# An encoder trunk's token mixer: conv output product as three one-pass products, attention block 1's last steps at fixed places, the LayerNorm's transposes in one row

## The chip, the cores and the metric

The kernel runs on one NeuronCore of a Trainium2 chip. The core has a matrix engine (TensorE, PE, with its weight loads PEld), a vector engine (VectorE, DVE), a scalar engine (ScalarE, ACT), a third elementwise engine (GpSimd, POOL), a queue for data movement (SyncE, SP), and DMA engines that bring data from memory (HBM). The engines run side by side, each works through its own list of instructions in order, and they wait for each other by semaphores. The metric is the device time of one launch in microseconds (us); less is better.

## What is computed

Two encoder layers on 256 tokens of width 1024, all float32. Cut to what the change touches:

```python
h = x + 0.5 * swiglu(rms_norm(x, norm_ffn1), w_ffn1_in, w_ffn1_out)
u = rms_norm(h, norm_mix)
q, k, v, c, g = split(u @ w_in)             # 512, 128, 128, 1024, 2048 columns
y_attn = window_attention(q, k, v, sink, rel_bias) @ w_attn_out     # 512 -> 1024
c = c_val * sigmoid(c_gate)                 # 512 channels
c = depthwise_conv(c, conv_w) + conv_b      # 31 taps
c = silu(layer_norm(c, conv_ln_g, conv_ln_b))
y_conv = c @ w_conv_out                     # 512 -> 1024
h = h + (sigmoid(g_attn) * y_attn + sigmoid(g_conv) * y_conv) @ w_o
h = h + 0.5 * swiglu(rms_norm(h, norm_ffn2), w_ffn2_in, w_ffn2_out)
x = h + (p @ w_pe_proj) * sigmoid(rms_norm(h, norm_pe) @ w_pe_gate)
```

The hidden width of swiglu is 2816. Nearly all of the arithmetic is products of 256 tokens with large weights.

## The kernel before

**Products.** Activations lie with their channels on the 128 partitions and the 256 tokens along the free dimension. A float32 product is run in one of two ways. The usual one (`mm3`, L312) splits both operands into a high part, rounded to the one-pass type fp32r, and a low part, the rest; it adds three one-pass products for each tile of 128 input channels: high by high (L318), high weights by low activations (L319), low weights by high activations (L320). The other way (`products`, L859, its matmul on L863) multiplies the float32 operands as they are; it is used for the attention output (tiles `ps_ao`), whose activation `o` isn't split, and for the conv output (`ps_co`), whose activation `y` isn't split.

**Weights.** The class `Weights` streams them. A load of up to 1 MB goes through SP into one of four buffers (`raw`, RAW_BUFS). From it come pieces ("specs"): ACT casts the high part (`w_hi`, L103), DVE takes the difference (`w_lo`, L104), into one of seven pairs of buffers. `get()` hands the next piece to the product and prepares up to LOOK = 6 pieces ahead, less `rest`. A raw spec has no preparation: its product reads the raw buffer, which is held until then.

**Order.** Each instruction has a priority by its place in the program (and offsets: `ws.lag` puts the weights' preparation 100 places later, `background` the taps of the convolution 800); from these and the dependencies a scheduler makes a fixed list for each engine. `tc.keep_in_program_order` ties an instruction to the one written ahead of it on its engine. `ws.later(n, fn)` calls a step when the n-th next piece of weights is fetched.

**The mixer** (`mix`, twice in a run) projects u to the conv branch (two halves times a sigmoid, into `cpad`), keys, values and queries, then 16 gate tiles in 8 pairs (`ps_g`, evicted by DVE on L844). The 31 taps for each of four channel groups run on DVE (L614) between other work. Attention goes in two blocks of 128 queries: `scores` (products, then the softmax), `attend` for each of two heads' groups (8 transposes into `ps_pt` on L807, copied by ACT to `pTs` on L811) and `gather` (`ps_o` on L819, copied to `o` on L827). `ws.later` puts these steps between the gate tiles.

Then come four groups of the attention output `attn_out` (16 matmuls into `ps_ao`, evicted by DVE on L873); among them the LayerNorm of `y`: `ln_by_token` turns y to tokens on partitions (8 transposes, `ps_yt`, L885), takes the statistics (L887, L888, L891) and normalises (`yn`, L894); `ln_by_channel` turns back (`ps_yc`, L904), and ACT applies Silu into `y` (L908). Four groups of the conv output `conv_out` follow; each is multiplied by its gate (L935), added to the attention branch (L936), and split into `ym_h` (ACT, L453) and `ym_l` (DVE, L454). The product with w_o (`ps_wo`) ends in `x` (DVE, L954); from each of its 8 tiles ACT makes the square (L408, which POOL sums on L409) and `xf0h` (L441), and DVE `xf0l` (L442): the two parts of the next FFN's input, whose products are `ps_gu`. In layer 1 the names are `xf1h` and `xf1l`.

## Time and profile before

| | |
|---|---|
| median of three runs | 1104.88 us (1104.81 to 1105.29) |
| the profiled execution | 1104.41 us |
| its span on the core | 1102.6 us |
| PE busy | 1087.8 us (99%), 9082 matmuls |
| DVE busy | 810.2 us (73%) |
| ACT busy | 611.1 us (55%) |
| POOL busy | 88.0 us (8%) |
| read from HBM | 200.53 MB, 183 GB/s over the span |
| granted PE clock | 1.00 |

The span is the time from the first to the last event that the profiler records on the core; the time of the launch is 1.8 us longer. A row of the timeline gives start and duration in us, engine, line and operation, the tile written and the tiles read, shapes and count, and in brackets how long the engine was idle just before and what ended the idle time. Rows with a count stand for so many instructions in a row. The matmuls overlap in the records: a one-pass product of 256 columns is shown with 0.28 us while the next one starts well before its end, so the distance between starts is what counts. A product with float32 operands is shown as two records.

### The profile page before, as it was taken

What the parts mean: (1) busy time and instruction counts of PE and PEld (TensorE: products, weight loads), DVE (VectorE), ACT (ScalarE), POOL (GpSimd) and SP (SyncE); (2) the same over time, 40 slices, a digit from 0 to 9 for tenths busy, and PEclk for the clock granted to TensorE, in tenths of its full rate; (3) what the DMA queues carried; (4) which work ended last, traced back from release to release, by engine and by line L of the source; (5) the groups of instructions that cost most, each with busy time, mean ns of one, the idle gap of its engine ahead of it and who ended that gap; (6) DMA issues with size and microseconds to landing.
All of it is one profiled execution on the core that took longest, in us unless ns stands there. A gap on an engine that the chain in (4) does not pass through costs nothing.

```text
span 1102.6 us, 21823 instructions
## 1 busy us (share of the span) xinstructions
PE 1087.8 (99%) x9082; PEld 1061.2 (96%) x9082; DVE 810.2 (73%) x1214; ACT 611.1 (55%) x1029; POOL 88.0 (8%) x123
## 2 busy tenths in 40 slices
PE   7999999999999999999999999999999999999998
PEld 7999999999889999999999999999988999999997
DVE  5877666799878767666887776669996887676664
ACT  6754445676547555445764444457764565554553
POOL 3000001211002000001110000113100110000110
PEclk9999999999999999999999999999999999999999
DMA  8776556566075565546556564566542675554541
GB/s 269 263 246 216 181 173 217 176 193 162 1 266 179 198 208 183 185 171 228 185 197 200 183 204 153 181 228 195 149 116 81 229 236 184 199 191 150 195 154 39
DMA packets 195695, 203.00 MB, mean 184 GB/s; under 512 B 3731, under 2 KB 188899, under 8 KB 195596
## 3 DMA queue, kind: packets, MB, share of 16 engines
q1 hardware_dynamic: 195564, 201.60, 55.4%
q8 instruction: 71, 1.16, 0.4%
q14 instruction: 28, 0.23, 0.1%
q10 hardware_dynamic: 32, 0.01, 0.0%
HBM read 200.53 MB, written 1.06 MB: 183 GB/s over the span
## 4 chain that ended last, share of the span: by engine, by line
PE 95%; DVE 3%; ACT 1%; DMA 0%; issue 0%; ACTq 0%
PE ps_gu L320 14%; PE ps_gu L319 14%; PE ps_gu L318 14%; PE ps_fo L319 7%; PE ps_fo L320 7%; PE ps_fo L318 7%; PE ps_g L318 3%; PE ps_g L320 3%; PE ps_g L319 3%; PE ps_co L863 3%; PE ps_ao L863 2%; DVE w_lo L104 2%; PE ps_c L318 1%; PE ps_pe L320 1%; PE ps_pe L318 1%; PE ps_c L320 1%
## 5 line engine op out<-in xcount | busy, mean ns | idle before, releaser
L104 DVE TENSOR_TENSOR w_lo<-raw,w_hi 128x1024 fp32r<-128x1024 f32 (+1 forms) x368 | 441.9, 1205 | 212.5 <-ACT w_hi L103 211.6
L103 ACT CAST w_hi<-raw 128x1024 fp32r<-128x1024 f32 (+1 forms) x368 | 379.2, 1036 | 377.4 <-PE ps_gu L319 195.4
L320 PE MATMUL ps_fo<-h_hi,w_lo 128*128 128x256 f32 x704 | 193.0, 275 | 0.0
L318 PE MATMUL ps_fo<-h_hi,w_hi 128*128 128x256 f32 x704 | 193.0, 275 | 0.0
L319 PE MATMUL ps_fo<-h_lo,w_hi 128*128 128x256 f32 x704 | 193.0, 275 | 0.0
L320 PEld LDWEIGHTS ps_fo<-h_hi,w_lo 128*128 128x128 f32 x704 | 131.8, 188 | 0.0
L318 PEld LDWEIGHTS ps_fo<-h_hi,w_hi 128*128 128x128 f32 x704 | 131.8, 188 | 0.0
L319 PEld LDWEIGHTS ps_fo<-h_lo,w_hi 128*128 128x128 f32 x704 | 131.8, 188 | 0.0
L409 POOL TENSOR_TENSOR sq_acc<-sq_acc,sq 128x256 f32<-128x256 f32 x56 | 56.0, 999 | 839.5 <-ACT sq L408 838.9
L614 DVE SCALAR_TENSOR_TENSOR y<-cpad,cw,y 128x256 f32<-128x256 f32 x240 | 101.3, 479 | 0.2
L318 PE MATMUL ps_gu<-x0h,w_hi 128*128 128x256 f32 x352 | 98.6, 280 | 2.0 <-ACT x L465 2.0
L320 PE MATMUL ps_gu<-x0h,w_lo 128*128 128x256 f32 x352 | 98.2, 279 | 0.2 <-DVE w_lo L104 0.2
L319 PE MATMUL ps_gu<-x0l,w_hi 128*128 128x256 f32 x352 | 98.0, 278 | 0.0
L319 PE MATMUL ps_gu<-xf0l,w_hi 128*128 128x256 f32 x352 | 97.2, 276 | 0.1
L319 PE MATMUL ps_gu<-xf1l,w_hi 128*128 128x256 f32 x352 | 97.2, 276 | 0.1
L318 PE MATMUL ps_gu<-xn0h,w_hi 128*128 128x256 f32 x352 | 97.0, 276 | 0.0
L318 PE MATMUL ps_gu<-xf0h,w_hi 128*128 128x256 f32 x352 | 97.0, 275 | 0.0
L318 PE MATMUL ps_gu<-xf1h,w_hi 128*128 128x256 f32 x352 | 97.0, 275 | 0.0
L320 PE MATMUL ps_gu<-xf0h,w_lo 128*128 128x256 f32 x352 | 96.9, 275 | 0.0
L320 PE MATMUL ps_gu<-xf1h,w_lo 128*128 128x256 f32 x352 | 96.9, 275 | 0.0
L320 PE MATMUL ps_gu<-xn0h,w_lo 128*128 128x256 f32 x352 | 96.8, 275 | 0.0
L319 PE MATMUL ps_gu<-xn0l,w_hi 128*128 128x256 f32 x352 | 96.8, 275 | 0.0
(225 smaller groups left out, 2646.4 us busy)
## 6 DMA issues: line engine op xcount, KB each, us to landing
raw<-in_w_ffn_in_dram SPq DMA_DIRECT2D x86, 1024.0 KB
raw<-in_w_in_dram SPq DMA_DIRECT2D x30, 1024.0 KB
raw<-in_w_ffn_out_dram SPq DMA_DIRECT2D x32, 896.0 KB
raw<-in_w_ffn_out_dram SPq DMA_DIRECT2D x16, 1024.0 KB
raw<-in_w_o_dram SPq DMA_DIRECT2D x8, 1024.0 KB
raw<-in_w_pe_gate_dram SPq DMA_DIRECT2D x8, 1024.0 KB
raw<-in_w_attn_out_dram SPq DMA_DIRECT2D x8, 512.0 KB
raw<-in_w_conv_out_dram SPq DMA_DIRECT2D x4, 1024.0 KB
```

The source lines that it names most:

```text
L103: nc.scalar.copy(out=hv[:, :, d0 : d0 + w], in_=src),
L104: nc.vector.tensor_tensor(out=lv[:, :, d0 : d0 + w], in0=src, in1=hv[:, :, d0 : d0 + w].bitcast(F32), op=ALU.subtract,),
L318: nc.tensor.matmul(ps, wh[:, k0 + k, cols], xh[:, kx, :], start=f, stop=False)
L319: nc.tensor.matmul(ps, wh[:, k0 + k, cols], xl[:, kx, :], start=False, stop=False)
L320: nc.tensor.matmul(ps, wl[:, k0 + k, cols], xh[:, kx, :], start=False, stop=e)
L409: nc.gpsimd.tensor_tensor(out=self.acc, in0=self.acc, in1=sq, op=ALU.add)
L614: nc.vector.scalar_tensor_tensor(out=y[:, i, :], in0=src, scalar=w, in1=y[:, i, :], op0=ALU.mult, op1=ALU.add)
L863: nc.tensor.matmul(ps[:, c * T : (c + 1) * T], w[:, k, c * P : (c + 1) * P], x[:, k, :], start=k == 0, stop=k == KC - 1,)
```

## The change

The edits, all in the mixer and in the weights' stream:

- **The conv output in three one-pass products.** The weights of `conv_out` become ordinary specs (a high and a low part, made by ACT and DVE), `y` is split after the Silu into `ys` (`y_h` by ACT, `y_l` by DVE, in two halves), and the product is `mm3`: 96 matmuls for each layer instead of 32 with float32 operands.
- **Attention block 1 at fixed places.** The two `attend` steps and `gather` of the second block of queries are no longer called by `ws.later`, but inside the last pair of gate tiles, between tied products: half of the first gate tile, both sets of transposes, the other half, two eighths of the second tile, gather, the rest. The sigmoids of the first 12 gate tiles come after that gather, and the copy to `o` is tied too.
- **LayerNorm's transposes together.** `ln_by_token` comes after two groups of the attention output, not after one, and its transposes and those of `ln_by_channel` are tied.
- **The weights' preparation held back.** From the last gate pair on, a preparation is issued only behind the last tap; from `ln_by_token` on, behind `yn`. `rest` is 2 from the first attention output to the product with w_o: four pieces ahead, not six.
- `RAW_BUFS` is 5, and a scratch area of the DMA (`dynamic_dma_scratch_size`) is set to 8192.

```diff
@@ -32,7 +32,8 @@
 LOOK = 6
-RAW_BUFS = 4
+RAW_BUFS = 5
+DMA_SCRATCH = 8192
 BACKGROUND = 800
@@ -53,7 +54,7 @@
         self.next_load = self.next_prep = self.next_get = 0
-        self.rest, self.pin, self.lag = 0, None, 0
+        self.rest, self.pin, self.lag, self.behind = 0, None, 0, None
     def unit(self, k, n, sources):
@@ -132,7 +133,8 @@
         self.tc.cur_priority = p0 + self.lag
-        self.prep_upto(i + LOOK - self.rest)
+        with self.tc.issue_after(self.behind) if self.behind else nullcontext():
+            self.prep_upto(i + LOOK - self.rest)
         self.tc.cur_priority = p0
@@ -274,7 +276,7 @@
             for c in range(2):
-                ws.raw_spec(u, KC, c * 256, 256)
+                ws.spec(KC, 256, [(u, 0, c * 256, 0, 256)])
         w = a["w_o"][l]
@@ -309,15 +311,16 @@
         return par[:, c0 + l * n + k : c0 + l * n + k + 1]
-    def mm3(ps, w, x, first=True, last=True, k0=0, x_k0=0, n_k=None, cols=slice(0, P)):
+    def mm3(ps, w, x, first=True, last=True, k0=0, x_k0=0, n_k=None, cols=slice(0, P), pin=False):
         (wh, wl), (xh, xl) = w, x
...
             f, e = first and k == 0, last and k == n_k - 1
-            nc.tensor.matmul(ps, wh[:, k0 + k, cols], xh[:, kx, :], start=f, stop=False)
-            nc.tensor.matmul(ps, wh[:, k0 + k, cols], xl[:, kx, :], start=False, stop=False)
-            nc.tensor.matmul(ps, wl[:, k0 + k, cols], xh[:, kx, :], start=False, stop=e)
+            for wa, xa, a, b in ((wh, xh, f, False), (wh, xl, False, False), (wl, xh, False, e)):
+                mm = nc.tensor.matmul(ps, wa[:, k0 + k, cols], xa[:, kx, :], start=a, stop=b)
+                if pin:
+                    tc.keep_in_program_order(mm)
     def pair(name, x, fresh):
@@ -602,6 +605,7 @@
             ws.lag = WEIGHTS_LAG
+            last_tap = [None]
             def tap(i, t):
@@ -611,7 +615,7 @@
                 else:
-                    nc.vector.scalar_tensor_tensor(
+                    last_tap[0] = nc.vector.scalar_tensor_tensor(
                         out=y[:, i, :], in0=src, scalar=w, in1=y[:, i, :], op0=ALU.mult, op1=ALU.add
                     )
@@ -805,7 +809,7 @@
                         turned = nc.tensor.transpose(ps[:, b, c, :], s[:, c, b * P : (b + 1) * P], ident)
-                        if (c, b) != (GROUP - 1, 0):
+                        if (c, b) != (GROUP - 1, 0) or qb == 1:
                             tc.keep_in_program_order(turned)
@@ -821,39 +825,67 @@
                         )
-                        if (b, v) != (0, 1):
+                        if (b, v) != (0, 1) or qb == 1:
                             tc.keep_in_program_order(mm)
                 ov = ps.rearrange("p (c q) -> p c q", c=GROUP)
-                nc.scalar.copy(out=o[:, :, qb * P : (qb + 1) * P], in_=ov[:, :, ::-1])
+                tc.keep_in_program_order(nc.scalar.copy(out=o[:, :, qb * P : (qb + 1) * P], in_=ov[:, :, ::-1]))
+                if qb == 1:
+                    for k in (0, 4, 8):
+                        squash(k)
             for at, fn in (
                 (0, lambda: scores(0)), (3, lambda: attend(0, 0)), (4, lambda: attend(0, 1)),
-                (6, lambda: scores(1)), (7, lambda: gather(0)), (9, lambda: attend(1, 0)),
-                (10, lambda: attend(1, 1)), (12, lambda: gather(1)),
+                (6, lambda: scores(1)), (7, lambda: gather(0)),
             ):
...
             g = mp.tile([P, 2 * KD, T], F32, name="g")
-            def gates(i):
-                ps, products = pair("ps_g", u, False)
+            def gates(i, products=None):
+                ps, whole_products = pair("ps_g", u, False)
                 def evac():
                     nc.vector.tensor_tensor(out=g[:, i : i + 2, :], in0=ps, in1=bcast(st.r, 2), op=ALU.mult)
-                group(products, evac)
+                group(products(ps) if products else whole_products, evac)
+
+            def last_gates(i):
+
+                def products(ps):
+                    w = []
+
+                    def some(c, k0, k1):
+                        if len(w) == c:
+                            w.append(ws.get())
+                        mm3(ps[:, c, :], w[c], u, first=k0 == 0, last=k1 == KD, k0=k0, x_k0=k0, n_k=k1 - k0, pin=True)
+
+                    def first():
+                        some(0, 0, KC)
+                        for v in range(2):
+                            attend(1, v)
+                        some(0, KC, KD)
+
+                    def second():
+                        some(1, 0, 2)
+                        gather(1)
+                        some(1, 2, KD)
+
+                    return [first, second]
+
+                gates(i, products)
             def squash(i):
...
                 tc.keep_in_program_order(nc.scalar.activation(out=gs, in_=gs, func=AF.Sigmoid))
             for i in range(0, 2 * KD, 2):
-                gates(i)
-                if i == 12:
-                    for k in (0, 4, 8):
-                        squash(k)
+                if i == 2 * KD - 2:
+                    ws.behind = last_tap[0].ins
+                    last_gates(i)
+                else:
+                    gates(i)
             def products(ps, x):
@@ -882,7 +914,8 @@
                     for i in range(KC):
-                        nc.tensor.transpose(ps[t][:, i * P : (i + 1) * P], y[:, i, t * P : (t + 1) * P], ident)
+                        turned = nc.tensor.transpose(ps[t][:, i * P : (i + 1) * P], y[:, i, t * P : (t + 1) * P], ident)
+                        tc.keep_in_program_order(turned)
                     six = tmp.tile([P, 6], F32, name="six")
@@ -891,28 +924,35 @@
                 for t in range(2):
-                    nc.vector.tensor_scalar(
+                    normed = nc.vector.tensor_scalar(
                         out=yn[:, t, :], in0=ps[t], scalar1=mv[:, t, 0:1], scalar2=rs[:, t : t + 1],
...
                     )
+                return normed.ins
+
+            ys = tuple(rows(mp, KC, "y_" + part) for part in "hl")
             def ln_by_channel():
...
                         for t in range(2):
-                            nc.tensor.transpose(
+                            turned = nc.tensor.transpose(
                                 ps[:, f, t * P : (t + 1) * P], yn[:, t, (i + f) * P : (i + f + 1) * P], ident
                             )
+                            tc.keep_in_program_order(turned)
                     for f in range(2):
...
                         )
+                    split(tuple(part[:, i : i + 2, :] for part in ys), y[:, i : i + 2, :])
             for i in range(KC):
-                if i == 1:
-                    ln_by_token()
+                if i == 0:
+                    ws.rest = 2
+                if i == 2:
+                    ws.behind = ln_by_token()
                 if i == 3:
@@ -937,7 +977,12 @@
                     split((yh[:, f % KC : f % KC + 2, :], yl[:, f % KC : f % KC + 2, :]), gs)
-                group([lambda: products(ps, y)], evac)
+                def products3():
+                    w = ws.get()
+                    for c in range(2):
+                        mm3(ps[:, c * T : (c + 1) * T], w, ys, cols=slice(c * P, (c + 1) * P))
+
+                group([products3], evac)
             for f in range(0, KD, 2):
@@ -972,7 +1017,7 @@
                 group([all_], evac)
-            ws.lag = 0
+            ws.lag, ws.rest, ws.behind = 0, 0, None
             mix_out(0, 2)
...
-    nc = bacc.Bacc("TRN2", target_bir_lowering=False, num_devices=1)
+    nc = bacc.Bacc("TRN2", target_bir_lowering=False, num_devices=1, dynamic_dma_scratch_size=DMA_SCRATCH)
```

What this moves shows in the engines' lists. First PE, from the attention output to the conv product in layer 0 (line, operation, tile written and read, shape, count; L885 and L917 are the LayerNorm's first transposes, L904 and L940 its second). Before:

```order
L863 MATMUL ps_ao<-o,raw 128x256 x8
L885 MATMUL ps_yt<-ident,y 128x128 x4
L863 MATMUL ps_ao<-o,raw 128x256 x3
L885 MATMUL ps_yt<-ident,y 128x128 x2
L863 MATMUL ps_ao<-o,raw 128x256 x5
L885 MATMUL ps_yt<-ident,y 128x128 x2
L863 MATMUL ps_ao<-o,raw 128x256 x8
L904 MATMUL ps_yc<-ident,yn 128x128 x8
L863 MATMUL ps_ao<-o,raw 128x256 x8
L863 MATMUL ps_co<-y,raw 128x256 x32
```

Now:

```order
L895 MATMUL ps_ao<-o,raw 128x256 x16
L917 MATMUL ps_yt<-ident,y 128x128 x8
L895 MATMUL ps_ao<-o,raw 128x256 x8
L940 MATMUL ps_yc<-ident,yn 128x128 x8
L895 MATMUL ps_ao<-o,raw 128x256 x8
L321 MATMUL ps_co<-y_h,w_hi 128x256 x3
L321 MATMUL ps_co<-y_l,w_hi 128x256
L321 MATMUL ps_co<-y_h,w_lo 128x256
```

The transposes moved behind the second group and stand together; one group lies between them and those that turn back. The first conv products are three that need only `y_h` and a high part of the weights; the fourth needs `y_l`. Ahead of this place the two sets of `ps_pt` transposes, which had 53 gate products behind the first set, now stand in one row of 16 with 36 behind them, 18 of these before `ps_o`. Behind it, the first two tiles of `ps_wo` were complete with the 74th of w_o's 192 products, and now with the 97th.

Second, DVE from the last taps to the split of y. Before (L104 is a low part of the weights):

```order
L614 SCALAR_TENSOR_TENSOR y<-cpad,cw,y 128x256 x5
L873 TENSOR_TENSOR g<-ps_ao,g 128x512 x2
L887 BN_STATS six<-ps_yt 128x6 x2
L888 BN_AGGR mv<-six 128x2 x2
L891 RECIPROCAL rs<-rs 128x2
L894 TENSOR_SCALAR yn<-ps_yt,mv,rs 128x512 x2
L873 TENSOR_TENSOR g<-ps_ao,g 128x512
L104 TENSOR_TENSOR w_lo<-raw,w_hi 128x1024 x2
L873 TENSOR_TENSOR g<-ps_ao,g 128x512
L104 TENSOR_TENSOR w_lo<-raw,w_hi 128x1024
```

Now (L105 is a low part of the weights):

```order
L618 SCALAR_TENSOR_TENSOR y<-cpad,cw,y 128x256 x2
L105 TENSOR_TENSOR w_lo<-raw,w_hi 128x1024 x2
L905 TENSOR_TENSOR g<-ps_ao,g 128x512
L920 BN_STATS six<-ps_yt 128x6 x2
L921 BN_AGGR mv<-six 128x2 x2
L924 RECIPROCAL rs<-rs 128x2
L927 TENSOR_SCALAR yn<-ps_yt,mv,rs 128x512 x2
L105 TENSOR_TENSOR w_lo<-raw,w_hi 128x1024 x4
L905 TENSOR_TENSOR g<-ps_ao,g 128x512
L105 TENSOR_TENSOR w_lo<-raw,w_hi 128x1024
L457 TENSOR_TENSOR y_l<-y,y_h 128x512 x2
```

Ahead of the first row shown stand six more taps and the first eviction of `ps_ao`. Between `yn` and `y_l` there are now four low parts, an eviction and a fifth low part; `y_l` itself is new.

Third, DVE where the product with w_o ends. Before:

```order
L954 TENSOR_TENSOR x_109<-ps_wo,x_109 128x256 x2
L104 TENSOR_TENSOR w_lo<-raw,w_hi 128x1024 x2
L954 TENSOR_TENSOR x_109<-ps_wo,x_109 128x256
L442 SCALAR_TENSOR_TENSOR xf0l<-x_109,par,xf0h 128x256 x2
L954 TENSOR_TENSOR x_109<-ps_wo,x_109 128x256
L104 TENSOR_TENSOR w_lo<-raw,w_hi 128x1024 x2
L442 SCALAR_TENSOR_TENSOR xf0l<-x_109,par,xf0h 128x256
L954 TENSOR_TENSOR x_109<-ps_wo,x_109 128x256
L442 SCALAR_TENSOR_TENSOR xf0l<-x_109,par,xf0h 128x256
L104 TENSOR_TENSOR w_lo<-raw,w_hi 128x1024
```

Now:

```order
L999 TENSOR_TENSOR x_109<-ps_wo,x_109 128x256 x2
L105 TENSOR_TENSOR w_lo<-raw,w_hi 128x1024
L999 TENSOR_TENSOR x_109<-ps_wo,x_109 128x256
L105 TENSOR_TENSOR w_lo<-raw,w_hi 128x1024
L445 SCALAR_TENSOR_TENSOR xf0l<-x_109,par,xf0h 128x256
L999 TENSOR_TENSOR x_109<-ps_wo,x_109 128x256
L445 SCALAR_TENSOR_TENSOR xf0l<-x_109,par,xf0h 128x256
L999 TENSOR_TENSOR x_109<-ps_wo,x_109 128x256
L105 TENSOR_TENSOR w_lo<-raw,w_hi 128x1024 x2
L445 SCALAR_TENSOR_TENSOR xf0l<-x_109,par,xf0h 128x256
L999 TENSOR_TENSOR x_109<-ps_wo,x_109 128x256
```

The kinds are the same in a slightly other sequence; from the first x to the seventh `xf0l` there are seven low parts in both, and seven x before, eight now.

## The prediction

> **What bounds the kernel now.** I read the page first: TensorE (PE) is busy 99% of the span, and the chain that ended last is 95% PE.

> ```profile
> span 1102.6 us, 21823 instructions
> PE 1087.8 (99%) x9082; PEld 1061.2 (96%) x9082; DVE 810.2 (73%) x1214; ACT 611.1 (55%) x1029; POOL 88.0 (8%) x123
> PE 95%; DVE 3%; ACT 1%; DMA 0%; issue 0%; ACTq 0%
> ```

> So the time falls only if PE gets less work or fewer gaps, and rises if a new gap opens. Then the stretches around the change, layer 0 (columns: stretch, length, busy and count of PE, PEld, DVE, ACT, POOL, clock, DMA share, GB/s):

> ```profile
> 275.00:295.00 20.00, 18.90 (x156) 17.24 (x155) 19.56 (x55) 14.34 (x33) 1.40 (x5) 1.00 0.01 2
> 295.00:311.00 16.00, 15.78 (x81) 13.45 (x80) 10.20 (x19) 7.74 (x10) 0.00 (x0) 1.00 0.20 66
> 311.00:325.00 14.00, 14.00 (x68) 12.37 (x67) 9.09 (x12) 6.27 (x7) 0.00 (x0) 1.00 0.90 303
> 325.00:350.00 25.00, 24.90 (x219) 24.70 (x219) 21.43 (x30) 15.11 (x27) 6.18 (x6) 1.00 0.64 220
> ```

> PE lacks 1.1 us in the first row and 0.3 in the rest. The column to watch is DVE: full until 295, and it gets the new work.

> **Work that goes: the conv product.** In the chain of waits (start, duration), 32 f32 products of 256 columns, each seen as two records, then the timeline's one-pass products, the first and the last of ten in a row:

> ```profile
> 310.93 13.81 PE ps_co L863 x64
> ...
> 345.24 0.28 PE L320 MATMUL ps_wo<-ym_h,w_lo 128*128 128x256 f32 x1
> ...
> 346.26 0.28 PE L320 MATMUL ps_wo<-ym_h,w_lo 128*128 128x256 f32 x1
> ```

> The spacing is (346.26 - 345.24)/9 = 0.1133 us. 96 one-pass products take 10.88 us instead of 13.81: 2.93 us less per layer.

> **Attention block 1 at fixed places.** Timeline before, PE's rows and then ACT's (in brackets the idle time before and what ended it):

> ```profile
> 283.52 1.03 PE L807 MATMUL ps_pt<-ident,s 128*128 128x128 f32 x8
> 284.31 0.36 PE L319 MATMUL ps_g<-xm0l,w_hi 128*128 128x256 f32 x1
> 284.98 1.03 PE L807 MATMUL ps_pt<-ident,s 128*128 128x128 f32 x8
> 287.12 1.94 PE L819 MATMUL ps_o<-pTs,vt 128*64 128x512 f32 x8 [1.10 <-ACT pTs L811]
> 294.58 0.59 PE L863 MATMUL ps_ao<-o,raw 128*128 128x256 f32 x2
> 281.42 1.71 ACT L799 ACTIVATE s<-s,den 128x256 f32<-128x256 f32 x4 [0.53 <-DVE den L797]
> 286.05 1.01 ACT L811 COPY pTs<-ps_pt 128x1024 f32<-128x1024 f32 x1 [0.44 <-PE ps_pt L807]
> 307.01 1.99 ACT L103 CAST w_hi<-raw 128x1024 fp32r<-128x1024 f32 x2 [0.93 <-DMA raw<-in_w_o_dram]
> ```

> A set of 8 transposes takes 0.8 to 0.9 us, so PE stood 1.27 us before ps_o. By the order, 53 gate products follow the first set now; after the change 36 will, so the sets start at 283.52 + 17 x 0.1133 = 285.45 and end at 287.1. 18 products (2.04) cover the two copies. The copies start at 286.3 and 287.3, and end by 288.3, before ps_o at 289.2. ACT must first fit five weight casts, which cost 0.96 each (1.99 for two, less overlap): one falls into its idle time, three delay the last normalising (283.04 now) by 2.9 less the 0.53 of its wait, to 285.3, and one runs until 286.3. The cover holds by 0.9 us; without it the old 1.27 returns. ps_ao starts near 293.2 instead of 294.58: 1.4 us gained.

> **What DVE must now do before the conv product can start.** DVE is in order. Its timeline before (columns as above):

> ```profile
> 285.79 8.80 DVE L614 SCALAR_TENSOR_TENSOR y<-cpad,cw,y 128x256 f32<-128x256 f32 x22
> 298.30 0.69 DVE L873 TENSOR_TENSOR g<-ps_ao,g 128x512 f32<-128x512 f32 x1 [0.48 <-PE ps_ao L863]
> 302.95 1.29 DVE L887 BATCH_NORM_STATS2 six<-ps_yt 128x6 f32<-128x512 f32 x2
> 306.46 0.68 DVE L873 TENSOR_TENSOR g<-ps_ao,g 128x512 f32<-128x512 f32 x1
> 308.09 2.36 DVE L104 TENSOR_TENSOR w_lo<-raw,w_hi 128x1024 fp32r<-128x1024 f32 x2 [0.95 <-ACT w_hi L103]
> ```

> Per instruction, with the overlap of neighbours taken off: a tap 0.40 (8.80/22), a w_lo 1.14 (2.36 for two), a 128x512 product or difference 0.60 (result after 0.68), statistics to the end of yn 306.46 - 302.95 = 3.51. As many taps remain as before. In the new order: the last gate eviction follows PE at 293.4; six taps to 296.4; the first ps_ao group is ready 3.72 after ps_ao starts (298.30 - 294.58), so at 296.9, and its eviction ends at 297.5; two taps, 298.3; two w_lo, 300.6; second eviction, 301.2; statistics and yn, 304.7. PE has its second group done at 300.3 and the eight transposes at 301.0, its third group (3.45) at 304.5: nearly no wait here.

> Now the order puts four w_lo, an eviction and a fifth w_lo ahead of y_l on DVE: 304.7 + 4 x 1.14 + 0.6 + 1.14 + 0.68 = 311.7. ACT's y_h is ready near 308.3 (ps_yc ends at 305.6; four Silu of 128x256 as the 1.71 above, two casts of half the 1.01), and the cast for the fifth w_lo near 305 (its 1.05 MB load can start when the second group frees a buffer, 300.3, and takes 3.5 us at the 303 GB/s of the third window), so neither decides. The second end of this estimate: before, the row of 307.01 shows a cast 0.93 late on such a load; as much here would still be before 311. PE is through with ps_yc and the last group at 309.0. It issues three products that need only y_h, one of them after an eviction at 309.8, and waits for y_l until 311.7: **a new wait of 2.4 us**.

> **What this delays.** With the first product that needs y_l, 93 conv products are left, and in the new order w_o's first tiles are complete with its 97th product, not the 74th. The last of these 190 starts 189 spacings after the first. So x0 can be evicted at 311.7 + 189 x 0.1133 + 0.33 = 333.4. Before, in DVE's timeline, with PE's and POOL's beside it:

> ```profile
> 333.20 0.76 DVE L954 TENSOR_TENSOR x<-ps_wo,x 128x256 f32<-128x256 f32 x2 [2.89 <-PE ps_wo L320]
> 337.76 2.89 DVE L104 TENSOR_TENSOR w_lo<-raw,w_hi 128x1024 fp32r<-128x1024 f32 x2
> 341.80 0.47 DVE L442 SCALAR_TENSOR_TENSOR xf0l<-x,par,xf0h 128x256 fp32r<-128x256 f32 x1
> 342.19 1.21 DVE L104 TENSOR_TENSOR w_lo<-raw,w_hi 128x1024 fp32r<-128x1024 f32 x1
> 347.77 0.96 DVE L442 SCALAR_TENSOR_TENSOR xf0l<-x,par,xf0h 128x256 fp32r<-128x256 f32 x1
> 348.66 0.41 DVE L954 TENSOR_TENSOR x<-ps_wo,x 128x256 f32<-128x256 f32 x1
> 346.37 0.28 PE L318 MATMUL ps_gu<-xf0h,w_hi 128*128 128x256 f32 x1
> 348.79 0.39 PE L319 MATMUL ps_gu<-xf0l,w_hi 128*128 128x256 f32 x1
> 347.71 0.74 POOL L409 TENSOR_TENSOR sq_acc<-sq_acc,sq 128x256 f32<-128x256 f32 x1 [2.01 <-ACT sq L408]
> ```

> From x0 to the end of the seventh xf0l DVE never rests: 333.20 to 348.66, 15.46 us for 7 x (0.33), 7 w_lo and 7 xf0l (0.39), which add up to 13.0. The other 2.5 is DVE slowed beside the six POOL sums of the fourth window, about 0.4 each: xf0l takes 0.96 instead of 0.47. PE's first product on the seventh xf0l (348.79) starts right behind it (347.77 + 0.96), 0.26 later than PE's own spacing would have it. The new order has the same 7 w_lo and 7 xf0l there, and 8 x instead of 7: 15.8 us, to 349.2. PE however finishes w_o already at 344.0 (311.7 + 285 x 0.1133) and runs dry at the sixth and seventh xf0l: **about 3.2 us of waiting**, resumed at 349.3 against 348.79.

> **Sum per layer.** Ahead of the conv product: 309.0 instead of 310.93, -1.93 (1.27 of it the old wait before ps_o, the rest small gaps and the copies' order); its own work -2.93; new wait +2.4; new wait +3.2 less the old 0.26 of the same kind: about +0.5 us, which is also 349.3 - 348.79, the difference of the two DVE chains. The FFN behind it is dense on PE and carries the shift to the end. Layer 1 repeats it 539.65 us later (row of the same product: 888.44). Two layers: +1.1 us. The profiled execution took 1104.41 (span 1102.6 and 1.8 around it), so 1105.5; the runs' median is 0.47 above it: **1106.0 us**.

> ```profile
> 888.44 0.39 PE L319 MATMUL ps_gu<-xf1l,w_hi 128*128 128x256 f32 x1
> ```

> The fifth raw buffer costs nothing: the loads it brings forward lie where DMA is idle (share 0.01 and 0.20 in the windows above), and casts in the FFN wait for PE's buffers. No row prices the smaller DMA scratch; the SP loads that it could touch keep DMA at 0.64 to 0.90 of its time in two windows and below 0.2 in the others, so I take nothing, and as its other end one load's 3.5 us, which the range covers.

> **Rivals.**
> *A, the DVE chains don't hold (faster).* If PE waits only for y_l, w_o ends at 344.0 and gate_up goes on, 2.4 to 2.7 us per layer are won: 1099.8. If neither wait comes, 2.93 + 1.4 per layer: 1096.2. For it: DVE is idle for 4.9 of the 14 us of the third window, into which the new work could slide. Against: DVE is in order, and every duration in the chain is a row of the same shape.
> *B, longer DVE chain (slower).* The place is the x0 to xf0l stretch. POOL's sums have to fall on two more short instructions there, 0.5 each (0.96 against 0.47): +1.0 per layer, 1108.0. It decides from +0.55 per layer on. For it: POOL sums bunch when x arrives in a burst. Against: there are six sums in both versions.
> *C, PE's clock drops in the longer gap (slower).* The first products of the run are 0.21 apart until 16.1 us, 5.4 us after they began; 5.4/0.21 = 25 such products cost 25 x 0.1 = 2.5 us per layer, 5 in all: 1111.

> ```profile
> 10.70 0.58 PE L318 MATMUL ps_gu<-x0h,w_hi 128*128 128x256 f32 x1 [2.04 <-ACT x L465]
> ...
> 15.90 0.41 PE L318 MATMUL ps_gu<-x0h,w_hi 128*128 128x256 f32 x1
> 16.11 0.36 PE L319 MATMUL ps_gu<-x0l,w_hi 128*128 128x256 f32 x1
> ```

> [...]
> *D, the change doesn't do what it says:* the split product isn't cheaper than 13.81. Then x0 comes at 311.7 + 13.81 - 0.34 + 97 x 0.1133 + 0.33 = 336.5, +3.3 per layer: 1111.5. For it: nothing but that no one-pass product of these operands is in the trace; against: ps_wo's have the same shape and spacing.

> **How the numbers follow.** Forecast 0.46, A 0.28 (its first form 0.18, its second 0.10), B 0.16, C 0.05, D 0.05. Under 0.2% (2.2 us, so 1102.7 to 1107.1) a measurement of this kernel doesn't tell from no change, so: faster 0.28, same 0.46, slower 0.26. The chain before y_l has eight DVE terms of rows that scatter by some 0.1 each, and the one before xf0l six collisions; +-1 per layer is the forecast's own range, 1103 to 1108. To hold the first form of A and B too, the range is 1099 to 1110; it leaves out A's second form, C and D.

> **What would show it.** Right: ps_co near 11 us of pure work but behind a PE wait for DVE's y_l of about 2 us; no wait before ps_o; x0 evicted within 0.5 us of 333.4; PE waiting about 3 us for xf0l at the start of the second FFN. Wrong: PE in 325 to 350 without a gap (A), or products 0.21 apart behind a gap (C).

## The result: slower, 1111.78 us, and the profile after

The changed kernel takes 1111.78 us (median of four runs, 1110.70 to 1112.29) against 1104.85 us for the kernel before beside it: 1.006 times the time, 95% interval 1.0048 to 1.0072. That is slower by little, but clear of the noise. I had forecast 1106.0 us, in a range of 1099 to 1110. The profiled execution of the changed kernel took 1112.29 us.

The page of the changed kernel, in the same rows as before (span, busy time by engine, chain that ended last by engine):

```profile
span 1110.4 us, 21980 instructions
PE 1088.0 (98%) x9146; PEld 1064.6 (96%) x9146; DVE 822.1 (74%) x1226; ACT 620.4 (56%) x1041; POOL 90.3 (8%) x123
PE 92%; DVE 5%; ACT 1%; DMA 1%; issue 1%; SPq 0%; ACTq 0%; DVEq 0%
```

PE is as long busy as before (1087.8), though it has 2.93 us less work in each layer. The stretches of layer 0 say why (stretch, length, busy and count of PE, PEld, DVE, ACT, POOL, granted PE clock, DMA share, GB/s):

```profile
275.00:295.00 20.00, 20.00 (x164) 18.36 (x163) 20.00 (x59) 17.11 (x37) 1.59 (x6) 1.00 0.01 3
295.00:311.00 16.00, 15.28 (x79) 13.18 (x77) 15.28 (x25) 9.42 (x13) 0.00 (x0) 1.00 0.50 165
311.00:325.00 14.00, 12.65 (x95) 12.45 (x96) 9.16 (x13) 4.32 (x6) 0.00 (x0) 0.88 0.74 254
325.00:350.00 25.00, 23.75 (x209) 23.55 (x207) 19.48 (x27) 14.86 (x25) 6.86 (x6) 1.00 0.46 152
350.00:360.00 10.00, 8.33 (x56) 8.27 (x57) 6.73 (x8) 4.78 (x7) 1.26 (x2) 0.83 0.56 185
...
310.60:314.00 3.40, 1.83 (x13) 1.63 (x14) 3.10 (x5) 0.00 (x0) 0.00 (x0) 1.00 1.06 375
314.00:317.40 3.40, 3.40 (x18) 3.40 (x18) 0.00 (x0) 0.00 (x0) 0.00 (x0) 0.50 1.08 383
317.40:320.80 3.40, 3.40 (x31) 3.40 (x31) 2.25 (x3) 1.89 (x3) 0.00 (x0) 1.00 0.16 50
```

The first row is better than before: PE is busy for all of it, where it lacked 1.1 us. From 311 on it is worse in two ways. PE stands (1.35 us in the third row, 1.25 in the fourth, 1.67 in the fifth), and the granted clock, 1.00 in the stretches of the kernel before, is 0.88 and 0.83. The last three rows take the first of these places apart: after 3.4 us in which PE was busy for only 1.83, the clock is 0.50 for 3.4 us and then 1.00 again.

PE's timeline, with the waits in brackets and the products behind them:

```profile
293.93 7.07 PE L895 MATMUL ps_ao<-o,raw 128*128 128x256 f32 x32
309.77 0.58 PE L321 MATMUL ps_co<-y_h,w_hi 128*128 128x256 f32 x2
310.82 0.38 PE L321 MATMUL ps_co<-y_h,w_hi 128*128 128x256 f32 x1 [0.46 <-DVE g L905]
312.56 0.39 PE L321 MATMUL ps_co<-y_l,w_hi 128*128 128x256 f32 x1 [1.35 <-DVE y_l L457]
...
314.97 0.41 PE L321 MATMUL ps_co<-y_h,w_lo 128*128 128x256 f32 x1
315.19 0.41 PE L321 MATMUL ps_co<-y_h,w_hi 128*128 128x256 f32 x1
...
351.67 0.58 PE L321 MATMUL ps_gu<-xf0l,w_hi 128*128 128x256 f32 x1 [2.92 <-DVE xf0l L445]
...
895.54 0.39 PE L321 MATMUL ps_gu<-xf1l,w_hi 128*128 128x256 f32 x1 [2.91 <-DVE xf1l L445]
```

The two waits stand where I had put them. Behind them the products come 0.21 us apart (314.97, 315.19) instead of 0.11 (called slow products from here on): 17 of them from 313.94, 14 from 351.67, 18 from 856.44 in layer 1. Behind the 2.91 us wait at 895.54 there are none. And DVE's timeline, the work ahead of y_l and the one from x to xf0l:

```profile
304.10 1.53 DVE L927 TENSOR_SCALAR yn<-ps_yt,mv,rs 128x512 f32<-128x512 f32 x2
305.55 4.62 DVE L105 TENSOR_TENSOR w_lo<-raw,w_hi 128x1024 fp32r<-128x1024 f32 x4
310.09 0.68 DVE L905 TENSOR_TENSOR g<-ps_ao,g 128x512 f32<-128x512 f32 x1
310.69 1.21 DVE L105 TENSOR_TENSOR w_lo<-raw,w_hi 128x1024 fp32r<-128x1024 f32 x1
311.82 1.29 DVE L457 TENSOR_TENSOR y_l<-y,y_h 128x512 fp32r<-128x512 f32 x2
...
336.09 0.76 DVE L999 TENSOR_TENSOR x<-ps_wo,x 128x256 f32<-128x256 f32 x2 [4.83 <-PE ps_wo L321]
...
351.14 0.47 DVE L445 SCALAR_TENSOR_TENSOR xf0l<-x,par,xf0h 128x256 fp32r<-128x256 f32 x1
351.53 0.41 DVE L999 TENSOR_TENSOR x<-ps_wo,x 128x256 f32<-128x256 f32 x1
351.87 0.47 DVE L445 SCALAR_TENSOR_TENSOR xf0l<-x,par,xf0h 128x256 fp32r<-128x256 f32 x1
352.26 1.21 DVE L105 TENSOR_TENSOR w_lo<-raw,w_hi 128x1024 fp32r<-128x1024 f32 x1
```

y_l was ready at 312.5 (I had 311.7), x was evicted from 336.09 (333.4), the xf0l on which PE waits, the sixth, ended at 351.61. DVE runs through from x to there, 15.5 us. The forecast's stretch went to the end of the seventh: from 336.09 to 352.26, where the next instruction starts, it is 16.2 us (I had 15.8).

By the first starts of tiles on PE, before and after: the conv product 310.77 and 309.77, w_o 324.39 and 324.90, gate_up 346.37 and 346.66, and the sum of squares after gate_up's first products (ps_stat) 351.67 and 356.48. So layer 0 loses 4.8 us, of which 0.54 stood before the mixer (by the first ps_stat ahead of the mixer, 200.29 and 200.83; in other profiled executions with the same buffers this start differs by -0.5 to +0.7 from the kernel before, and the 0.54 lies within that), and layer 1 another 3.0 (ps_stat 891.32 and 899.13).

### The profile page after: what moved, and what is told of

It reads as the page before. It is cut to its first block, busy times and chain, and to the rows that moved or that the text cites. A ratio compares the mean times of both kernels' runs of the same rounds, so it can differ in the third digit from the quotient of the medians.

```text
span 1110.4 us, 21980 instructions
## 1 busy us (share of the span) xinstructions
PE 1088.0 (98%) x9146; PEld 1064.6 (96%) x9146; DVE 822.1 (74%) x1226; ACT 620.4 (56%) x1041; POOL 90.3 (8%) x123
## 4 chain that ended last, share of the span: by engine, by line
PE 92%; DVE 5%; ACT 1%; DMA 1%; issue 1%; SPq 0%; ACTq 0%; DVEq 0%
PE ps_gu L321 43%; PE ps_fo L321 22%; PE ps_g L321 8%; PE ps_c L321 4%; PE ps_pe L321 4%; DVE w_lo L105 3%; PE ps_co L321 2%; PE ps_wo L321 2%; PE ps_pp L321 1%; PE ps_s L767 1%; ACT g L881 1%; PE ps_o L823 1%; PE ps_q L726 1%; PE ps_q L727 1%; PE ps_q L728 1%; PE ps_pt L811 1%
## 5 line engine op out<-in xcount | busy, mean ns | idle before, releaser
L104 ACT CAST w_hi<-raw 128x1024 fp32r<-128x1024 f32 (+1 forms) x376 | 388.3, 1037 | 387.4 <-PE ps_gu L321 200.4
L105 DVE TENSOR_TENSOR w_lo<-raw,w_hi 128x1024 fp32r<-128x1024 f32 (+1 forms) x376 | 452.2, 1208 | 200.3 <-ACT w_hi L104 200.3
L412 POOL TENSOR_TENSOR sq_acc<-sq_acc,sq 128x256 f32<-128x256 f32 x56 | 58.4, 1043 | 843.3 <-ACT sq L411 842.6
```

Of the source, the lines that this page charges most:

```text
L104: nc.scalar.copy(out=hv[:, :, d0 : d0 + w], in_=src),
L105: nc.vector.tensor_tensor(out=lv[:, :, d0 : d0 + w], in0=src, in1=hv[:, :, d0 : d0 + w].bitcast(F32), op=ALU.subtract,),
L412: nc.gpsimd.tensor_tensor(out=self.acc, in0=self.acc, in1=sq, op=ALU.add)
```

## The experiments

Theory: the time goes in the two waits and in the slow products behind them, and both come from the split conv product. Rivals: another part of the change costs it (buffers, places, held-back preparation); the clock drops for a reason other than idle time; DVE's volume, and not the order, decides. The kernel before lay between 1104.6 and 1105.2 us beside each of the runs that follow; ratios are to it, with their 95% intervals. Differences in us between runs are differences of medians, and carry these 0.6 us.

**The change without the split.**

```diff
-                ws.spec(KC, 256, [(u, 0, c * 256, 0, 256)])
+                ws.raw_spec(u, KC, c * 256, 256)
...
-                group([products3], evac)
+                group([lambda: products(ps, y)], evac)
```

> The change without its first part: the conv output goes back to float32 operands and raw weights, the fixed places, the transposes together, the held-back preparation and the buffers stay. Theory (the time is lost in two waits of PE, for y_l and for xf0l, and in the slow products behind each; all come from the split): no wait and no slow products in the conv product, no wait of 3 us at the second FFN; conv product starts some 1 us earlier than before the change, so 1102.9 us, 1101.5 to 1104.5. Rival (the buffers, the scratch or the attention's places cost it): 1108 or more.

Measured: 1099.88 us, 0.9953 of the kernel before (0.9936 to 0.9970). PE's timeline shows no wait in either mixer, and the granted clock is 1.00. Two rows of it by stretch:

```profile
311.00:325.00 14.00, 14.00 (x76) 12.61 (x75) 10.67 (x15) 5.52 (x7) 0.00 (x0) 1.00 0.93 320
325.00:350.00 25.00, 25.00 (x222) 24.95 (x221) 18.81 (x25) 15.52 (x26) 6.41 (x7) 1.00 0.57 194
```

The direction of the theory holds and the rival falls: all but the split is a gain of 5.3 us (1105.21 us beside it), more than I expected, and the split, which takes 2.9 us of PE's work from each layer, costs 1111.78 - 1099.88 = 11.9 us.

**The split alone**, on the kernel before: conv weights as pieces with two parts, y split, `mm3` for the product, and nothing else.

> The kernel before with the first part of the change alone: conv weights split, y split, three one-pass products. Theory: DVE has no low parts ahead of y_l here, but the LayerNorm's transposes come later; y_l near 312.4, a wait of 2 to 2.5 us at the conv product, x evicted at 334 to 336, end of the xf0l chain 350 to 351.6: 1107 to 1111 us. Rival (the one-pass products help by themselves and the other parts cost the time): 1099 to 1103.

Measured: 1132.37 us, 1.0242 (1.0224 to 1.0261). Far worse than either side expected. In DVE's timeline:

```profile
291.85 5.63 DVE L614 SCALAR_TENSOR_TENSOR y<-cpad,cw,y 128x256 f32<-128x256 f32 x14
297.41 1.21 DVE L104 TENSOR_TENSOR w_lo<-raw,w_hi 128x1024 fp32r<-128x1024 f32 x1
...
306.46 0.47 DVE L614 SCALAR_TENSOR_TENSOR y<-cpad,cw,y 128x256 f32<-128x256 f32 x1
...
310.63 1.53 DVE L894 TENSOR_SCALAR yn<-ps_yt,mv,rs 128x512 f32<-128x512 f32 x2
...
321.16 1.29 DVE L454 TENSOR_TENSOR y_l<-y,y_h 128x512 fp32r<-128x512 f32 x2 [2.11 <-ACT y_h L453]
```

The scheduler, which sees new preparations of weights, puts them among the taps; the last tap ends at 306.9, yn at 312.2, and y_l comes at 321 to 322, ten microseconds later than in the full change. PE waits 3.45 us for yn and 2.20 for y_h. With the first of these the granted clock falls to 0.50 for 6.83 us (310.60 to 317.43), and DVE waits 6.20 us, to 318.36, for PE's ps_ao. So the other parts of the change are what makes the split bearable at all; my 334 to 336 for x assumed the LayerNorm's old place.

**Attention's places alone**, on the kernel before.

> The kernel before with the second part of the change alone: attention block 1 at fixed places inside the last pair of gate tiles. My forecast's term: the wait before ps_o (1.10 us) goes and ps_ao starts 1.4 us earlier in each layer, 1104.7 - 2.8 = 1101.9 us, 1101 to 1103. Rival (the LayerNorm's transposes have no part in the gain that the change without the split shows): 1099 to 1100.5. Rival (without the held-back preparation the scheduler puts low parts among the taps, and the LayerNorm comes late): above 1104.

Measured: 1106.67 us, 1.0021 (1.0011 to 1.0030). The time is the one of the third expectation, but not its cause. ps_o no longer waits and ps_ao starts at 293.32, as in the full change, but PE then waits 1.86 us for yn, and the conv product starts at 311.44, later than before (310.77): the 1.26 us that ps_ao had won are gone again. DVE's rows, and PE's wait:

```profile
294.13 2.58 DVE L615 SCALAR_TENSOR_TENSOR y<-cpad,cw,y 128x256 f32<-128x256 f32 x6
302.93 1.30 DVE L915 BATCH_NORM_STATS2 six<-ps_yt 128x6 f32<-128x512 f32 x2 [1.14 <-PE ps_yt L913]
306.59 0.41 PE L932 MATMUL ps_yc<-ident,yn 128*128 128x128 f32 x2 [1.86 <-DVE yn L922]
```

No low part stands among the taps, and the last tap ends at 298.6, as in the change without the split (298.5). The LayerNorm is late because DVE waits for PE: the transposes still lie scattered among the products of the attention output, the last two at 302.62, where in the change without the split all eight are through by 301.1. So by these rows what this part lacks alone is the LayerNorm's transposes in one row, not the held-back preparation; no run adds the transposes by themselves.

**The waits filled, first form.** Products that nobody reads stand in for idle time: 20 ahead of the conv product, 24 in the second FFN. The rest of the program is the change's.

```diff
+    def extra(n, a, b):
+        spare = at_tile("ps_spare")
+        for _ in range(n):
+            tc.keep_in_program_order(nc.tensor.matmul(spare[:, :T], a, b, start=True, stop=True))
...
                     w = ws.get()
+                    if f == 0:
+                        extra(20, w[0][:, 0, 0:P], w[0][:, 1, :])
```

> The changed kernel with products that nobody reads put into PE's two waits of each layer: 20 one-pass products (2.3 us) ahead of the conv product, 24 (2.7 us) ahead of the eighth's eighth of the first gate_up products. They take the place of idle time, and make the waits no shorter. Theory (idle time of 1.8 and 2.9 us makes PE's clock drop, which costs the 1.6 us of slow products behind it, three times in the run): no products 0.21 apart behind the waits, 1111.8 - 4.8 = 1107.0 us, 1106 to 1108.5. Rival (the clock drops for another reason, as the load on PE or DMA): the slow products stay, 1111 to 1112.5. Rival (the waits are longer than the filling, so that it only delays): above 1112.5.

Measured: 1115.76 us, 1.0096 (1.0081 to 1.0111). It answers half the question. At the conv product the filling took the wait's place: the rows

```profile
309.63 2.74 PE L328 MATMUL ps_spare<-w_hi 128*128 128x256 f32 x20
312.20 0.52 PE L321 MATMUL ps_co<-y_h,w_hi 128*128 128x256 f32 x3
312.56 0.28 PE L321 MATMUL ps_co<-y_l,w_hi 128*128 128x256 f32 x1
```

show the first product with y_l at 312.56, exactly where it was in the change, but no slow products follow there, and w_o starts at 323.14 instead of 324.90. In the second FFN I had put the 24 products behind the first product that waits, not ahead of it; there they added their 2.7 us to a wait that stayed (2.91 us), and so did the slow products behind it.

**The waits filled, mended.** The 24 products now ahead of the sixth eighth of the first gate tile.

> As the filled waits before (20 products ahead of the conv product), but the 24 products at the second FFN now stand ahead of the first product that waits there (the sixth eighth of the first gate tile). Theory (part of the loss is PE's slow clock behind idle time): no products 0.21 apart at either place; the first sum of squares on PE (ps_stat) at 353.5 instead of 356.5 in layer 0; 1111.8 - 4.9 = 1106.9 us, 1105.5 to 1108.5. Rival (the clock drops for another reason): slow products stay, 1111 to 1113.

Measured: 1106.98 us, 1.0020 (1.0011 to 1.0029), as expected, ps_stat at 353.17 in layer 0 and no slow products at either place:

```profile
345.81 2.93 PE L328 MATMUL ps_spare<-xf0h,w_hi 128*128 128x256 f32 x24
349.02 0.38 PE L321 MATMUL ps_gu<-xf0l,w_hi 128*128 128x256 f32 x1 [0.16 <-DVE xf0l L456]
```

PE does more here, none of it useful, and the kernel is 4.8 us faster than the change (4.5 us if each is taken against the kernel before beside it, 6.9 and 2.4 us above it). That part of the loss is the slow clock alone, and idle time is what brings it on.

**Waits and the clock by themselves.** Another program, in one execution: groups of 84 to 112 products, between them waits of 12 lengths made by copies on ACT.

> Not the trunk: 84 groups of 84 to 112 one-pass products of 256 columns, between which PE waits for a chain of copies on ACT, of 12 lengths (near 1.2 to 3.8 us), 7 times each; the output is zeros and a piece of the last copy. It measures after what gap the products come 0.21 apart. [...] If it is the busy share of a window that runs on its own, gaps of 2 to 3 us are followed by them in some cases and not in others, by where they fall, with slow stretches of about one length, and their starts are whole numbers of one period apart.

PE's timeline gives start, duration and count of a group and the wait ahead of it. Two pairs of equal groups:

```profile
196.71 12.85 PE L39 MATMUL ps<-r,w 128*128 128x256 f32 x105 [0.91 <-ACT r L45]
264.33 14.35 PE L39 MATMUL ps<-r,w 128*128 128x256 f32 x105 [1.94 <-ACT r L45]
...
132.77 15.13 PE L39 MATMUL ps<-r,w 128*128 128x256 f32 x112 [2.58 <-ACT r L45]
280.83 13.70 PE L39 MATMUL ps<-r,w 128*128 128x256 f32 x112 [2.15 <-ACT r L45]
```

A group is either as long as after a short wait or about 1.5 us longer. Over the 83 waits between groups:

```
wait, us          0.91  1.08  1.30  1.51  1.72  1.94  2.15  2.36  2.58  2.79  3.00  3.22
groups            7     7     7     7     7     7     7     7     7     7     7     6
of them longer    0     0     0     0     5     5     4     5     5     3     6     5
```

No wait up to 1.51 us is followed by a drop of the clock; from 1.72 us on 38 of 55 are, hardly more often at 3.2 than at 1.7. Nearly all of them cost 1.5 us (1.24 to 1.51; two near 2.7). The trace's record of the granted clock shows the stretches of half clock themselves, 39 with the one at the program's end. Their starts are whole numbers of 3.413 us apart, to within 0.003 us, and each lasts one such stretch, or two behind the two waits that cost 2.7. If time is cut by this grid, every drop follows a stretch with at least 1.72 us of idle time, and no stretch with more than 1.80 us kept the clock; seven between 1.65 and 1.80 did. So the expectation holds in this program: stretches of 3.413 us that run on their own, and 1.72 to 1.80 us idle in one of them, about half, was enough.

**y_l first.** The preparation from the last attention output on waits for y_l, not for yn.

```diff
-                    ln_by_channel()
+                    ws.behind = ln_by_channel()      # now returns the last y_l
```

> The changed kernel with the weights' preparation from the fourth attention output on held back behind y_l instead of yn: one low part and an eviction stand between yn and y_l on DVE, not five low parts and one eviction (the others follow y_l). Theory: y_l ends 1.9 us earlier (it starts when y_h is there, 309.9), PE waits under 1 us, no slow products in the conv product, x evicted 3.7 us earlier, the wait at the second FFN stays near 3 us: 1111.8 - 2 x 3.7 = 1104.4 us, 1103 to 1107. Rival (the wait for y_l only moves into one for the low parts of the conv weights): 1110 to 1112.

Measured: 1109.26 us, 1.0040 (1.0025 to 1.0055): a gain of 2.5, not 7.4. The wait for y_l is gone and there are no slow products in the conv product; x comes at 333.14 instead of 336.09. But the wait for xf0l stayed, in two pieces:

```profile
347.12 0.58 PE L321 MATMUL ps_gu<-xf0l,w_hi 128*128 128x256 f32 x1 [1.71 <-DVE xf0l L445]
347.50 0.41 PE L321 MATMUL ps_gu<-xf0h,w_lo 128*128 128x256 f32 x1
347.71 0.41 PE L321 MATMUL ps_gu<-xf0h,w_hi 128*128 128x256 f32 x1
348.65 0.58 PE L321 MATMUL ps_gu<-xf0l,w_hi 128*128 128x256 f32 x1 [0.52 <-DVE xf0l L445]
```

and in both layers some 28 products behind it are slow (in layer 0 up to 353.9, where the clock returns to 1.00): two stretches of half clock, where the change had one in layer 0 and none in layer 1. What the wait gave, the clock took.

**The same with that wait filled** (20 products).

> The run with y_l first, and 20 products that nobody reads ahead of the first product that waits for xf0l in each layer's second FFN. Theory (of the 4.4 us by which that run lies above the kernel before, the slow clock behind the wait is the larger part; 28 products in each layer came 0.1 us late): no slow products there, 1109.3 - 5.6 = 1103.7 us, 1102.5 to 1105. Rival (the wait itself is what costs): 1107 to 1110.

Measured: 1107.82 us, 1.0031 (1.0018 to 1.0043), its runs from 1105.93 to 1111.06. Inconclusive, though the time lies in the rival's range: PE waited 1.72 us one eighth earlier than where I had put the filling, which then stood behind the wait; in the profiled execution its 20 products took 4.00 us, at the slow clock.

**Without POOL's sums** over the mixer's x.

> The changed kernel without POOL's sums of squares over the x of the mixer (only the first square is kept, so the second FFN's norm is not the reference's). Theory (in the stretch from x to xf0l DVE is the bound, and 2.5 us of it are DVE's instructions slowed beside POOL's sums): the sixth xf0l ends near 349.2 instead of 351.6, PE waits about 0.6 us instead of 2.9, no slow products behind it, those in the conv product stay: 1111.8 - 6.2 = 1105.6 us, 1104.5 to 1107. Rival (the weights' casts, which wait for free buffers, set the end of the stretch): 1110 to 1112.

Measured: 1102.49 us, 0.9980 (0.9970 to 0.9990). In DVE's timeline, the first x and the sixth xf0l:

```profile
335.20 0.76 DVE L1002 TENSOR_TENSOR x<-ps_wo,x 128x256 f32<-128x256 f32 x2 [4.83 <-PE ps_wo L321]
347.45 0.48 DVE L446 SCALAR_TENSOR_TENSOR xf0l<-x,par,xf0h 128x256 fp32r<-128x256 f32 x1
```

From x to the sixth xf0l DVE now takes 335.20 to 347.92, 12.7 us instead of 15.5; PE does not wait there at all, and in both layers only the slow products of the conv product are left. The gain is 9.3 us, more than the 6.2 expected, since the wait went wholly, not to 0.6. That POOL's sums lengthen this stretch by 2.8 us is shown; the sums are needed, so this is a measurement and not a version.

**w_o's order written out**, with y_l first: the first halves of tiles 0 to 4, then the second halves of tiles 0 and 1.

> The changed kernel with y_l first (as in the run before), and PE's order in the product with w_o written out and tied: the first halves of tiles 0 to 4, then the second halves of tiles 0 and 1, then the rest, so that the first two x are complete with the 84th product, not the 99th, and nothing is put between. Theory (the wait at the second FFN is long because x starts late against PE, which DVE then cannot make up): x evicted near 330.5 instead of 333.1, the wait for xf0l under 0.5 us, no slow products there: 1109.3 - 9 = 1100 us, 1098.5 to 1102. Rival (the volume of DVE's work in this stretch decides, the low parts come no earlier): 1106 to 1109.

Measured: 1109.87 us, 1.0045 (1.0028 to 1.0061). No gain. A first half needs both pieces of the first ym_l, and the second of these ended only at 326.6 (DVE is busy without a break from 310 to 328.6); PE waited 2.90 us for it, and 23 products behind that wait were slow.

**The same by quarters**: the first two eighths of tiles 0 to 4, then the next two, then the second halves of tiles 0 and 1.

```diff
-                for f in range(WO_AHEAD):
-                    wo_part(f, 0, KC)
+                for k in (0, 2):
+                    for f in range(WO_AHEAD):
+                        wo_part(f, k, k + 2)
```

> As the run with w_o's order written out, but by quarters: products of the first two eighths of tiles 0 to 4, then of the next two, then the second halves of tiles 0 and 1, so that PE has 30 products before it needs the second ym_l. Theory (that run lost by PE's wait of 2.9 us for that ym_l and the slow products behind it): this wait under 1 us, x evicted about 1 us earlier than with y_l first alone, the wait for xf0l about 1 us and no slow products behind it: 1105 us, 1103 to 1107. Rival (DVE's volume decides): 1108 to 1110.

Measured: 1100.63 us, 0.9964 (0.9951 to 0.9977), better than expected: the split kept, and 11 us faster than the change. Its rows by stretch:

```profile
311.00:325.00 14.00, 13.35 (x118) 13.15 (x117) 14.00 (x17) 5.88 (x7) 0.00 (x0) 1.00 0.95 315
325.00:350.00 25.00, 23.84 (x208) 23.45 (x207) 20.52 (x29) 14.54 (x25) 6.79 (x7) 1.00 0.50 172
```

PE still stands 1.8 us in these two rows, in pieces of 0.2 to 0.8 (the longest, 0.79, for xf0l), and the clock stays at 1.00. Against the run with y_l first, the waits shrink by some 1 us in each layer and the slow products, 28 in each layer, go: together 8.6 us. DVE is busy for all of the first row; without the split (above) it was for 10.67 of 14. The two versions are not told apart by their times (0.9953, 0.9936 to 0.9970 without the split): with the split PE has 5.9 us less work in the two layers, and none of that can be seen in the time.

## Why the prediction was wrong

**The step that failed.** The sum priced PE's two new waits as idle time and nothing more; the half clock behind them stood at nothing in it, and only in rival C, at 0.05. The runs showed three stretches of half clock behind the four waits, 1.5 us each, 4.5 to 4.8 us in all (the change against the mended filling, in which they are gone). That is most of what lies between the forecast of 1106.0 and the measured 1111.78.

I gave C 0.05 because I assumed that waits of 2.4 and 3.2 us would leave the clock at 1.00; no run shows that, and it held for the wait of 2.91 us at 895.54 but not for the others: 310.60 to 314.00 was busy for 1.83 us of 3.40 and was followed by clock 0.50, and in the program of groups and waits 1.72 us were enough in five cases of seven.

C's own time, 1111, is nearly what was measured, in part by luck: the price I had put on a drop, 2.5 us, was taken from the first products of the run, 0.21 us apart from 10.70 to 16.11, of which the trace does not show that they ran at half clock, and is too high against the 1.5 us measured; and I had counted one drop in each layer, two in all, where three came.

**What bounds the kernel; the conv product.** Right. The split product costs what one-pass products cost: in the first filled run it takes 312.20 to 323.14, 10.9 us, against 13.6 before by the same count of starts.

**Attention block 1.** Right in the full change: no wait before ps_o, and ps_ao 1.2 us earlier (293.93 less the 0.54 of the start, against 294.58); I had 1.4. Alone it would have been worth nothing (1106.67): its gain came only together with the other parts, by the rows of that run above all the LayerNorm's transposes in one row. That dependence I didn't see.

**The wait for y_l.** Right in place and cause, four low parts, an eviction and a fifth. y_l at 312.5 instead of 311.7, 0.54 of it the start; PE idle 1.8 us instead of 2.4, since PE came 0.2 us later and the three products cover a part.

**x and the wait for xf0l.** Right in mechanism and close in size: 2.92 us against 3.2, and DVE's 16.2 us to the seventh xf0l against 15.8. But x came at 336.09 instead of 333.4: 0.54 from the start, 0.3 from y_l, and 1.7 from slow products, which the term didn't have.

**The sum without the slow clock.** It was close, not exact: the mended filling lies 2.4 us above the kernel before beside it (1.2 to 3.2 by its interval), where I had 1.1. The longer DVE stretch (0.4) and the later y_l (0.3) in each layer would make about that difference; this is an estimate from the rows above, not a measurement.

**Rival A** fell by both waits. **B** came nearer than its time suggests: it needed over 16.3 us from x to the seventh xf0l, and 16.2 was measured. **D** fell by the 10.9 us.

## What to carry to other kernels

A change that takes work from the busiest engine is to be priced against the engines that must feed it: here 2.9 us less on PE meant some 6 us more on DVE (four low parts at 1.14, two halves of y_l at 0.6), in a stretch where DVE had 4.9 us to spare, and the order then decided whether it paid (1111.8, 1109.3, 1109.9, 1100.6 us for the same work on PE). As far as these runs show, PE's idle time within any 3.41 us, the length of the half-clock stretches here, is to be kept under 1.5 us, all pieces taken together: 0.46 and 1.35 us close to each other halved the clock (0.50 from 313.98); in the program of groups and waits none of the 28 waits up to 1.51 us was followed by a drop, and those from 1.72 us on cost another 1.5 us in 38 cases of 55. The parts of a joint change need not add up: attention alone +2 us, the split alone +27, both with the rest +7, all but the split -5.

## What the runs showed of the hardware that I had not expected

```profile
348.11:351.52 3.41, 0.64 (x6) 0.44 (x4) 3.41 (x4) 1.75 (x3) 0.73 (x1) 1.00 1.10 384
890.84:894.25 3.41, 1.79 (x15) 1.58 (x14) 3.41 (x5) 1.75 (x3) 1.16 (x2) 1.00 1.08 379
894.25:897.66 3.41, 2.01 (x15) 1.81 (x15) 3.41 (x6) 1.79 (x3) 0.84 (x1) 1.00 0.53 187
```

  The first wait left 2.77 us of one stretch idle; the second was divided over two, 1.62 and 1.40 us, and the clock stayed at 1.00. The exact limit stays open: 1.60 us idle in 310.57 to 313.98 did halve the clock, and among float32 products and transposes 1.86 us left it at 1.00 twice (304.10 to 307.51 with attention's places alone, 317.43 to 320.84 with the split alone).
- In the changed kernel half clock lasted one such stretch each time, with PE busy for 3.42 of 3.42 us from 313.98, 3.26 of 3.41 from 351.52 and 3.41 of 3.41 from 856.70. It lasted two with y_l first, where 0.53 us of idle time in the half-clock stretch from 347.11 was followed by another stretch at 0.50. What decides that stays open. That the wider scatter of runs with such waits (1105.93 to 1111.06 in one) comes from where the waits fall is likely and not shown; in that run the three slowest executions have mean clocks of 0.995 and 0.996, the four fastest 0.997 to 1.000.
- Products that compute nothing of use, put into idle time, made the kernel 4.8 us faster than the change without them.
- DVE's short instructions beside POOL's sums: without the seven sums of the mixer's x, six of which fall into this stretch, 15.5 us of DVE's work took 12.7.
